# Keys turned by VectorE and moved through DRAM in a two-layer hybrid decoder kernel

## The chip, the cores and the metric

One core of a Trainium2 chip runs the kernel. The metric is device time in microseconds of one execution. The core has TensorE (PE, matrix products, with PEld for loading the stationary operand), VectorE (DVE), ScalarE (ACT), GpSimd (POOL) and SyncE (SP); SP here does nothing but issue transfers (DMAs). PE writes only to PSUM, the other engines work on SBUF and PSUM.

## The reference

Two layers over x (256 tokens, width 1024, f32). Each layer normalises x, projects it by `w_in` to ten parts of 512 columns, runs three branches, multiplies by a SiLU gate and projects back by `w_out`:

```python
h = rms_norm(x, norm_g[l])
q_a, k_a, v_a, q_h, f_h, i_h, q_m, z = split(h @ w_in[l])
qa = partial_rope(rms_norm(q_a), positions); ka = partial_rope(rms_norm(k_a), positions)
o_a = moba_attention(qa, ka, va)       # 8 heads x 64; with 256 tokens one block: causal softmax attention
o_h = rms_norm(hgrn2_chunkwise(q_h, f_h, i_h, lb))           # 4 heads x 128, gated recurrence
k_m, v_m = split(rms_norm(mem) @ w_mem_kv[l])                # 256 memory tokens
o_m = memory_attention(rms_norm(q_m), rms_norm(k_m), v_m)    # 4 heads x 128, softmax
x = x + (concat(o_a, o_h, o_m) * silu(z)) @ w_out[l]
```

All of it is in f32 accuracy.

## The kernel before, in words

**Products.** To get f32 accuracy from fp32r products, both operands of a large product are split into a high and a low part (`wh` by ACT at L161/L164, `wl` by DVE at L173/L176), and three products are summed. A weight chunk is 128 x 1024 (512 KB). It is loaded into one of four raw buffers (`wr`, L136), split into one of three `wh` and `wl` buffers, and used by 12 or 16 products of 512 columns (L215; L1136 for `w_out`). There are 120 chunks in a fixed order: per layer the memory's k and v (8), HGRN's f and q (4 + 4), then k of MoBA, i of HGRN, q of MoBA, the HGRN gate, q of the memory branch, v of MoBA, two more gates (4 each), and `w_out` (12).

**Slots.** The weight products form the backbone. After every six products (in some groups after six and ten) `slot()` is called. It lets each side job, a Python generator, go one step; `yield n` means that a job comes back after n slots. So the order in which the program is written out follows the products. From that order the framework's scheduler sets the order on each engine by a simulated timeline; only the products written with `mm_row`, the loads of weights and a few others are kept in program order among themselves.

**Side jobs that matter here.**
- `g_km` normalises the memory's keys in `kn` (buffer tag `qk`, one buffer, used next by `kr` of MoBA's k) at L600. PE then turns them in two groups of four transposes (L611) into PSUM; ACT takes the high part `kmh` (L612), DVE the low part `kml` (L613). `g_mem_unit` reads them as the moving operand of its scores (12 fp32r products of 256 columns per unit, two units per layer).
- `g_qk` normalises and rotates MoBA's k and q in `kr`; k is scaled at L909, both are turned by PE at L919 and copied out by ACT at L920, into `kT` and `qT`.
- `g_moba` computes the first scores (L219, 8 products of 128 columns and 4 of 256) and starts two units. `g_moba_unit` computes for the second unit its own scores (4 products of 256), takes exps (L967), and passes the probabilities `P` to `across`.
- `across` is the way that P goes already: DVE turns 32 x 32 blocks (L92) into `blk`, one store brings `blk` to a DRAM tile `there` (L96), and four loads bring it back (L99) so that the blocks stand where a full transpose wants them, as `PT`. The columns of PT are in the order (partition quarter, head and token half, 32 tokens), so the PV products read it in runs of 32 columns (L994).
- `room`, `take` and `rel` count buffers: four PSUM tiles `sd` for side products, two buffers `P`, one each of `PTh`, `PTl` and `blk`. The memory units wait for `P`, then for `sd`, then for `PTh` and `PTl`.
- `g_hgrn` runs the recurrence in several levels: DVE scales (L760, L761, L777), PE multiplies in small products (L219).

**SP's queue.** SP issues transfers in order. The weight loads, each waiting until its raw buffer is free, share it with the stores and loads of `across`.

Of the kernel before, what the change touches and what calls it, by code (L numbers as in the profile page):

```python
# [12 lines left out]
F32 = mybir.dt.float32  # L13
F32R = mybir.dt.float32r
# [31 lines left out]
def hymba_kernel(ctx: ExitStack, tc: tile.TileContext, x, mem, mem_t, positions, w_in, w_out, w_mem_kv,  # L46
                 gains, moba_g, out):
    nc = tc.nc
# [15 lines left out]
    def room(what, n=1):  # L64
        while held[what] + n > room_of[what]:
            yield
# [9 lines left out]
    def side_tile():  # L76
        held["sd"] += 1
        assert held["sd"] <= 4
        return psum.tile([128, 512], F32, name="sd", tag="sd", bufs=4)

    def rel(what="sd", n=1):
        held[what] -= n
# [2 lines left out]
        return sb.tile([128, n], F32, name=name, tag=name, bufs=2)  # L85


    def across(dst, src, n):
        yield from room("blk")
        held["blk"] += 1  # L90
        blk = sb.tile([128, 4, n * 32], F32, name="blk", tag="blk", bufs=1)
        nc.vector.transpose(blk.rearrange("p c (n i) -> p c n i", n=n),  # L92
                            src.rearrange("p (n c i) -> p c n i", n=n, c=4))
        yield 2
        there = away.tile([4, 32, 4, n * 32], F32, name="there", tag="there", bufs=2)
        nc.sync.dma_start(there.rearrange("q j c r -> (q j) c r"), blk)  # L96
        yield 2
        for c in range(4):
            nc.sync.dma_start(dst[c * 32:c * 32 + 32], there[:, :, c].rearrange("q j r -> j q r"))  # L99
            if c % 2:  # L100
                yield
        rel("blk")

    chunks = []

# [473 lines left out]
    def g_km(l, acc):  # L579
        ss = small("ssk", 8)  # L580
        kn = sb.tile([128, 2, 512], F32, name="kn", tag="qk", bufs=1)
        nc.vector.tensor_copy(kn[:, 0], acc[0])
        nc.scalar.copy(kn[:, 1], acc[1])  # L583
        yield
        for t in range(2):
            sumsq(ss[:, t * 4:t * 4 + 4], kn[:, t], 4)
        yield
        while "rm" not in done:
            yield
        ms = small("msk", 8)  # L590
        for t in range(2):
            nc.vector.tensor_scalar(ms[:, t * 4:t * 4 + 4], ss[:, t * 4:t * 4 + 4], rm2[:, t:t + 1], EPS,
                                    op0=OP.mult, op1=OP.add)
        r = small("rk", 8)
        nc.gpsimd.tensor_tensor(r, ms, pw[:, :8], op=OP.pow)
        for t in range(2):
            nc.gpsimd.tensor_scalar(r[:, t * 4:t * 4 + 4], r[:, t * 4:t * 4 + 4], rm[:, t:t + 1], None, op0=OP.mult)
        yield 3
        for t in range(2):
            nc.vector.tensor_tensor(heads(kn[:, t], 4), heads(kn[:, t], 4),  # L600
                                    r[:, t * 4:t * 4 + 4][:, :, None].to_broadcast([128, 4, 128]), op=OP.mult)
        yield 3
        kmh = sb.tile([128, 4, 256], F32R, name="kmh", tag="kmh", bufs=1)
        kml = sb.tile([128, 4, 256], F32R, name="kml", tag="kml", bufs=1)
        g = gkq[:, l:l + 1]
        for t in range(2):
            ts = slice(t * 128, (t + 1) * 128)
            yield from room("sd")
            pt = side_tile()
            for h in range(4):  # L610
                nc.tensor.transpose(pt[:, h * 128:(h + 1) * 128], kn[:, t, h * 128:(h + 1) * 128], ident)  # L611
            nc.scalar.activation(kmh[:, :, ts], heads(pt, 4), AF.Copy, scale=g)  # L612
            nc.vector.scalar_tensor_tensor(kml[:, :, ts], in0=heads(pt, 4), scalar=g, in1=kmh[:, :, ts].bitcast(F32),  # L613
                                           op0=OP.mult, op1=OP.subtract)
            rel()
        T["km"] = kmh, kml
        done.add(f"km{l}")

# [259 lines left out]
    def g_qk(l, q, acc):  # L878
        ss = small("ssa", 16)
        ms = small("msa", 16)  # L880
        r = small("rka" if q else "rqa", 16)
        kr = sb.tile([128, 2, 512], F32, name="kr", tag="qk", bufs=1)
        for t in range(2):
            t8 = slice(t * 8, t * 8 + 8)
            sumsq(ss[:, t8], acc[t], 8)
            nc.vector.tensor_scalar(ms[:, t8], ss[:, t8], 1.0 / 64, EPS, op0=OP.mult, op1=OP.add)
            nc.gpsimd.tensor_tensor(r[:, t8], ms[:, t8], pw[:, :8], op=OP.pow)
            a3 = heads(acc[t], 8)
            k3 = heads(kr[:, t], 8)
            nc.vector.tensor_tensor(k3, a3, rtA[:, l, q, t][:, None, :].to_broadcast([128, 8, 64]), op=OP.mult)  # L890
            tm = sb.tile([128, 8, 16], F32, name="tm", tag="tm", bufs=2)
            nc.vector.tensor_tensor(tm[:, :, 0:8], a3[:, :, 8:16],
                                    rtB[:, l, q, t][:, None, 0:8].to_broadcast([128, 8, 8]), op=OP.mult)
            nc.vector.tensor_tensor(tm[:, :, 8:16], a3[:, :, 0:8],
                                    rtB[:, l, q, t][:, None, 8:16].to_broadcast([128, 8, 8]), op=OP.mult)
            yield
            nc.vector.tensor_tensor(k3[:, :, 0:16], k3[:, :, 0:16], tm, op=OP.add)
            yield
        if q == 0:
            rq = small("rq", 16)  # L900
            nc.gpsimd.tensor_scalar(rq, r, 0.125, None, op0=OP.mult)
            nr = small("nr", 16)
            nc.gpsimd.tensor_scalar(nr, r, -0.125, None, op0=OP.mult)
            T["rq"], T["nr"] = rq, nr
        else:
            yield
            for t in range(2):
                k3 = heads(kr[:, t], 8)
                nc.vector.tensor_tensor(k3, k3, r[:, t * 8:t * 8 + 8][:, :, None].to_broadcast([128, 8, 64]),  # L909
                                        op=OP.mult)  # L910
                yield
        yield 2
        tg = ("qT", "kT")[q]
        o = sb.tile([128, 4, 256], F32, name=tg, tag=(f"yl{M_}", f"yh{M_}")[q], bufs=1)
        for t in range(2):
            yield from room("sd")
            pt = side_tile()
            for p in range(4):
                nc.tensor.transpose(pt[:, p * 128:(p + 1) * 128], kr[:, t, p * 128:(p + 1) * 128], ident)  # L919
            nc.scalar.copy(o[:, :, t * 128:(t + 1) * 128], heads(pt, 4))  # L920
            rel()
            yield
        T[tg] = o
        if q == 0:
            spawn(g_moba(l))
# [10 lines left out]
    def second(u):  # L936
        qT, kT = T["qT"], T["kT"]
        ps = [side_tile() for _ in range(2)]
        for pi in range(2):
            for e in range(2):  # L940
                mm_row(ps[e][:, pi * 256:(pi + 1) * 256], qT[64 * e:64 * e + 64, 2 * u + pi, 128:256],
                       kT[64 * e:64 * e + 64, 2 * u + pi])
        return ps

    def second_masked(u, ps, P, mx):
# [5 lines left out]
    def g_moba_unit(l, u, P, mx):  # L951
# [26 lines left out]
        tag = ("PTh", "PTl")[u]  # L978
        yield from take(tag)
        PT = sb.tile([128, 4, 384], F32, name="PT", tag=tag, bufs=1)  # L980
        yield from across(PT, P.rearrange("p i s -> p (i s)"), 12)
        rel("P")
        yield 5
        while f"va{l}" not in done or f"z{A_}{l}" not in done:
            yield
        va = T["va"]
# [13 lines left out]
    def g_moba(l):  # L1000
        T.pop(f"y{A_}", None)
        qT, kT = T["qT"], T["kT"]
        yield
        yield from room("P", 2)
        held["P"] += 2
        P = [sb.tile([128, 4, 384], F32, name="P", tag="P", bufs=2) for _ in range(2)]
        mx = [small("mxa%d" % u, 8) for u in range(2)]

        yield from room("sd", 4)
        ps = [side_tile() for _ in range(2)]  # L1010
        for p in range(4):
            for e in range(2):
                mm_row(ps[e][:, p * 128:(p + 1) * 128], qT[64 * e:64 * e + 64, p, 0:128],
                       kT[64 * e:64 * e + 64, p, 0:128])
        ps1 = second(0)
        yield
        for p in range(4):
            for e in range(2):
                masked(P[p // 2], p % 2 * 2 + e, 0, ps[e][:, p * 128:(p + 1) * 128], mx[p // 2])
        rel("sd", 2)  # L1020
        second_masked(0, ps1, P[0], mx[0])
        for u in range(2):
            yield 1 + 2 * u
            spawn(g_moba_unit(l, u, P[u], mx[u]))


# [28 lines left out]
    def g_mem_unit(l, u, qm, r, nr):  # L1055
# [7 lines left out]
        for t in range(2):  # L1063
            for i in range(2):
                for a, b in passes:
                    mm(ps[t][:, i * 256:(i + 1) * 256], qm[a][:, 2 * u + i, t * 128:(t + 1) * 128],
                       km[b][:, 2 * u + i], (a, b) == passes[0], (a, b) == passes[2])
        yield
        mx = small("mxm%d" % u, 4)
        nb = small("nbm%d" % u, 4)  # L1070
# [181 lines left out]
```

## Time and profile before

| What | Value |
|---|---|
| Median of 3 runs | 402.9 us (402.66 to 403.1) |
| Profiled execution | 402.69 us, span 400.9 us, granted PE clock 1.00 |
| PE, DVE, ACT, POOL busy | 394.4, 309.7, 266.1, 56.7 us |
| DMA | 74.06 MB, 185 GB/s mean |

A row of the groups gives line, engine, operation, what it writes and reads, shape and count, then busy time and the mean of one in ns, then the idle time before the group with what ended it. A row of the chain gives start, duration and what ran. A wait reads "who waits <- for whom: total, times, longest".

### The profile page before, as it was taken

The numbers are of one execution on the slowest core, as the hardware profiler recorded it, in microseconds if no ns is written. First come the engines' busy times: TensorE is split into PE (matmuls) and PEld (weight loads), VectorE is DVE, ScalarE is ACT, GpSimd is POOL, SyncE is SP. The second block draws the span as 40 slices with busy tenths as digits, with TensorE's granted clock in tenths as the row PEclk, the third lists the DMA queues.
The fourth block names the chain that finished last, engine by engine and source line by source line (L and its number), as shares of the span: only waits on it lengthen the run. The fifth ranks groups of instructions, "written<-read, shape, count | busy, mean of one in ns | idle before, by whom it ended". The sixth has DMA issues, their size and how long they took to land.

```text
span 400.9 us, 7637 instructions
## 1 busy us (share of the span) xinstructions
PE 394.4 (98%) x2919; PEld 330.3 (82%) x2919; DVE 309.7 (77%) x602; ACT 266.1 (66%) x438; POOL 56.7 (14%) x79
## 2 busy tenths in 40 slices
PE   8999999999999999999999999999999999999996
PEld 6888888888788888888888888888888889878885
DVE  4789999977559896885576789799656798789643
ACT  5998746584775969864466676456755868897340
POOL 2013405406001200000000040040150040000000
PEclk9999999999999999999999999999999999999999
DMA  8976453355435779337664555544454285953612
GB/s 287 412 276 230 175 180 138 125 199 206 140 115 205 225 252 221 113 115 239 188 194 160 202 163 202 175 146 159 159 171 146 79 261 213 250 194 107 209 54 105
DMA packets 22629, 74.06 MB, mean 185 GB/s; under 512 B 2752, under 2 KB 5184, under 8 KB 22592
## 3 DMA queue, kind: packets, MB, share of 16 engines
q1 hardware_dynamic: 22304, 73.41, 54.7%
q8 instruction: 23, 0.38, 0.4%
q10 hardware_dynamic: 288, 0.15, 0.2%
q14 instruction: 14, 0.11, 0.1%
HBM read 69.36 MB, written 4.19 MB: 183 GB/s over the span
## 4 chain that ended last, share of the span: by engine, by line
PE 95%; ACT 2%; DMA 1%; SPq 0%; DVE 0%; issue 0%; ACTq 0%; DVEq 0%
PE acc L215 66%; PE acc L1136 16%; PE sd L215 5%; PE sd L219 4%; DMA wr<-in_w_mem_kv_dram 1%; ACT P L1081 1%; PE sd L919 1%; PE sd L428 1%; PE sd L1099 1%; ACT wh L161 0%; PE sd L731 0%; PE sd L611 0%; PE sd L1045 0%; SPq L136 0%; ACT wh L164 0%; DVE xs L1170 0%
## 5 line engine op out<-in xcount | busy, mean ns | idle before, releaser
L173 DVE TENSOR_TENSOR wl<-wr,wh 128x1024 fp32r<-128x1024 f32 x104 | 126.4, 1220 | 49.7 <-ACT wh L161 49.5
L161 ACT CAST wh<-wr 128x1024 fp32r<-128x1024 f32 x104 | 109.0, 1051 | 71.7 <-PE acc L215 52.9
L215 PE MATMUL acc<-wh,hT 128*128 128x512 f32 x384 | 126.3, 397 | 0.0
L215 PEld LDWEIGHTS acc<-wh,hT 128*128 128x128 f32 x384 | 72.0, 188 | 16.0 <-issue 0.7
L215 PE MATMUL acc<-wl,hT 128*128 128x512 f32 x192 | 75.1, 391 | 0.0
L215 PE MATMUL acc<-hT,wh 128*128 128x512 f32 x256 | 65.5, 395 | 0.0
L215 PEld LDWEIGHTS acc<-hT,wh 128*128 128x128 f32 x256 | 45.9, 189 | 8.4 <-ACT kn L583 0.4
L215 PEld LDWEIGHTS acc<-wl,hT 128*128 128x128 f32 x192 | 36.1, 188 | 6.7
L1136 PE MATMUL acc<-wl,yh 128*128 128x512 f32 (+1 forms) x96 | 37.2, 387 | 0.0
L215 PEld LDWEIGHTS acc<-hT,wl 128*128 128x128 f32 x256 | 34.8, 190 | 2.5 <-issue 0.3
L1136 PE MATMUL acc<-wh,yl 128*128 128x512 f32 (+1 forms) x96 | 36.8, 387 | 0.0
L215 PE MATMUL acc<-hT,wl 128*128 128x256 f32 x256 | 36.2, 283 | 0.0
L1136 PE MATMUL acc<-wh,yh 128*128 128x512 f32 (+1 forms) x96 | 31.5, 389 | 0.0
L164 ACT ACTIVATE wh<-wr,gT 128x1024 fp32r<-128x1024 f32 (+1 forms) x21 | 19.4, 945 | 9.8 <-PE acc L215 4.0
L215 PE MATMUL acc<-wh,mTh 128*128 128x512 f32 x64 | 25.2, 396 | 0.4 <-ACT wh L164 0.2
L176 DVE SCALAR_TENSOR_TENSOR wl<-wr,gT,wh 128x1024 fp32r<-128x1024 f32 (+1 forms) x21 | 21.0, 1027 | 5.7 <-ACT wh L164 5.5
L215 PE MATMUL acc<-wh,mTl 128*128 128x512 f32 x64 | 24.8, 390 | 0.0
L967 ACT ACTIVATE P<-P,nba,rq 128x128 f32<-128x128 f32 (+1 forms) x32 | 17.1, 538 | 7.1 <-DVE nba L961 7.1
L1136 PEld LDWEIGHTS acc<-wh,yl 128*128 128x128 f32 x96 | 18.0, 188 | 3.7
L1136 PEld LDWEIGHTS acc<-wl,yh 128*128 128x128 f32 x96 | 18.0, 188 | 3.6
L1136 PEld LDWEIGHTS acc<-wh,yh 128*128 128x128 f32 x96 | 17.9, 188 | 3.5
L215 PE MATMUL acc<-wl,mTh 128*128 128x512 f32 x64 | 20.2, 392 | 0.0
(221 smaller groups left out, 584.4 us busy)
## 6 DMA issues: line engine op xcount, KB each, us to landing
wr<-in_w_in_dram SPq DMA_DIRECT2D x80, 512.0 KB, 3.3
wr<-in_w_out_dram SPq DMA_DIRECT2D x24, 512.0 KB, 4.4
wr<-in_w_mem_kv_dram SPq DMA_DIRECT2D x15, 512.0 KB, 4.6
there<-blk SPq DMA_DIRECT2D x4, 768.0 KB, 3.5
PT<-there SPq DMA_DIRECT2D x16, 192.0 KB, 5.9
xs<-in_x_dram SPq DMA_DIRECT2D x2, 512.0 KB, 8.9
memr<-in_mem_dram SPq DMA_DIRECT2D x2, 512.0 KB, 6.7
out_dram<-xs SPq DMA_DIRECT2D x3, 256.0 KB, 2.0
```

Of the source, the lines that this page charges most:

```text
L161: nc.scalar.copy(whs[i], raws[i])
L164: nc.scalar.activation(whs[i][:, sl], raws[i][:, sl], AF.Copy, scale=gT[:, g:g + 1])
L173: nc.vector.tensor_tensor(wls[i], raws[i], whs[i].bitcast(F32), op=OP.subtract)
L176: ins = nc.vector.scalar_tensor_tensor(wls[i][:, sl], in0=raws[i][:, sl], scalar=gT[:, g:g + 1], in1=whs[i][:, sl].bitcast(F32), op0=OP.mu ...
L215: nc.tensor.matmul(o, lhsT=a, rhs=b, start=s, stop=e)
L219: tc.keep_in_program_order(nc.tensor.matmul(o, lhsT=a, rhs=b, start=True, stop=True))
L428: ins = nc.tensor.transpose(pt[:, j * 256 + t * 128:j * 256 + (t + 1) * 128], xn[t][:, k * 128:(k + 1) * 128], ident)
L919: nc.tensor.transpose(pt[:, p * 128:(p + 1) * 128], kr[:, t, p * 128:(p + 1) * 128], ident)
L967: nc.scalar.activation(P[:, i, kc[t]], P[:, i, kc[t]], AF.Exp, bias=nb[:, c:c + 1], scale=rq[:, r:r + 1], accum_out=sm[:, c:c + 1])
L1081: nc.scalar.activation(P[:, t, i], ps[t][:, i * 256:(i + 1) * 256], AF.Exp, bias=nb[:, c:c + 1], scale=r[:, cr:cr + 1], accum_out=sm[:, c: ...
L1099: nc.tensor.transpose(pt[:, i * 256 + t * 128:i * 256 + (t + 1) * 128], P[:, t, i, b * 128:(b + 1) * 128], ident)
L1136: ins = nc.tensor.matmul(a, lhsT=y, rhs=wt[:, cs], start=n == (0 if to is None else nk - 2) and j == 0, stop=n == nk - 1 and j == 2)
```

## The change

1. `kn` isn't turned by PE any more. DVE turns its 32 x 32 blocks, the result goes through DRAM and comes back into `kn` itself (`turned`); then one ACT instruction of 1024 columns makes `kmh` and one DVE instruction makes `kml`.
2. MoBA's k goes the same way into `kT`; q is still turned by PE.
3. Columns of `kmh`, `kml` and `kT` are now in the order (token quarter, token half, head, 32 tokens). The scores pick them by `strips`, in runs of 32 columns, so that the scores themselves stand as before.
4. `across` gives its buffers back sooner: `P` after DVE's transpose, `blk` after the store is written out. Between store and loads there are 4 slots instead of 2, and the four loads go out in two steps.
5. The second MoBA unit starts one slot after the first instead of three, which is twelve products earlier.

```diff
-    def across(dst, src, n):
-        yield from room("blk")
-        held["blk"] += 1
-        blk = sb.tile([128, 4, n * 32], F32, name="blk", tag="blk", bufs=1)
+    def across(dst, src, n, stage=None, free=None):
+        if stage is None:
+            yield from room("blk")
+            held["blk"] += 1
+        tag = stage or "blk"
+        blk = sb.tile([128, 4, n * 32], F32, name="blk", tag=tag, bufs=1)
         nc.vector.transpose(blk.rearrange("p c (n i) -> p c n i", n=n),
                             src.rearrange("p (n c i) -> p c n i", n=n, c=4))
+        if free is not None:
+            rel(free)
         yield 2
         there = away.tile([4, 32, 4, n * 32], F32, name="there", tag="there", bufs=2)
         nc.sync.dma_start(there.rearrange("q j c r -> (q j) c r"), blk)
-        yield 2
+        if stage is None:
+            rel("blk")
+        yield 4
         for c in range(4):
             nc.sync.dma_start(dst[c * 32:c * 32 + 32], there[:, :, c].rearrange("q j r -> j q r"))
-            if c % 2:
+            if c == 1:
                 yield
-        rel("blk")
+
+    def turned(a, stage=None):
+        yield from across(a.rearrange("p (q r) -> p q r", q=4), a, 8, stage)
+        yield 5
+
+    def strips(a):
+        return a.rearrange("p (q t h i) -> p h t q i", q=4, t=2, h=4)
...
@@ g_km
-        kmh = sb.tile([128, 4, 256], F32R, name="kmh", tag="kmh", bufs=1)
-        kml = sb.tile([128, 4, 256], F32R, name="kml", tag="kml", bufs=1)
+        kmh = sb.tile([128, 1024], F32R, name="kmh", tag="kmh", bufs=1)
+        kml = sb.tile([128, 1024], F32R, name="kml", tag="kml", bufs=1)
         g = gkq[:, l:l + 1]
-        for t in range(2):
...
-                nc.tensor.transpose(pt[:, h * 128:(h + 1) * 128], kn[:, t, h * 128:(h + 1) * 128], ident)
-            nc.scalar.activation(kmh[:, :, ts], heads(pt, 4), AF.Copy, scale=g)
-            nc.vector.scalar_tensor_tensor(kml[:, :, ts], in0=heads(pt, 4), ...)
-            rel()
+        flat = kn.rearrange("p t s -> p (t s)")
+        yield from turned(flat)
+        nc.scalar.activation(kmh, flat, AF.Copy, scale=g)
+        nc.vector.scalar_tensor_tensor(kml, in0=flat, scalar=g, in1=kmh.bitcast(F32), op0=OP.mult, op1=OP.subtract)
...
@@ g_qk
+        flat = kr.rearrange("p t s -> p (t s)")
+        o = sb.tile([128, 1024], F32, name=tg, tag=(f"yl{M_}", f"yh{M_}")[q], bufs=1)
+        if q == 0:
...
+        else:
+            yield from across(o.rearrange("p (q r) -> p q r", q=4), flat, 8)
+            yield 5
...
@@ second
-                mm_row(ps[e][:, pi * 256:(pi + 1) * 256], qT[64 * e:64 * e + 64, 2 * u + pi, 128:256],
-                       kT[64 * e:64 * e + 64, 2 * u + pi])
+                mm_row(ps[e][:, pi * 256:(pi + 1) * 256].rearrange("p (t q i) -> p t q i", t=2, q=4),
+                       qT[64 * e:64 * e + 64, 2 * u + pi, 128:256], strips(kT)[64 * e:64 * e + 64, 2 * u + pi])
...
@@ g_moba_unit
-        yield from across(PT, P.rearrange("p i s -> p (i s)"), 12)
-        rel("P")
-        yield 5
+        yield from across(PT, P.rearrange("p i s -> p (i s)"), 12, free="P")
+        yield 6
...
@@ g_moba
-                mm_row(ps[e][:, p * 128:(p + 1) * 128], qT[64 * e:64 * e + 64, p, 0:128],
-                       kT[64 * e:64 * e + 64, p, 0:128])
+                mm_row(ps[e][:, p * 128:(p + 1) * 128].rearrange("p (q i) -> p q i", q=4),
+                       qT[64 * e:64 * e + 64, p, 0:128], strips(kT)[64 * e:64 * e + 64, p, 0])
...
         for u in range(2):
-            yield 1 + 2 * u
+            yield
             spawn(g_moba_unit(l, u, P[u], mx[u]))
...
@@ g_mem_unit
-                    mm(ps[t][:, i * 256:(i + 1) * 256], qm[a][:, 2 * u + i, t * 128:(t + 1) * 128],
-                       km[b][:, 2 * u + i], (a, b) == passes[0], (a, b) == passes[2])
+                    mm(ps[t][:, i * 256:(i + 1) * 256].rearrange("p (t q s) -> p t q s", t=2, q=4),
+                       qm[a][:, 2 * u + i, t * 128:(t + 1) * 128], strips(km[b])[:, 2 * u + i],
+                       (a, b) == passes[0], (a, b) == passes[2])
```

More of the change, by code (lines that the diff above doesn't have):

```diff
@@ L602, in g_km @@
         yield 3
-        kmh = sb.tile([128, 4, 256], F32R, name="kmh", tag="kmh", bufs=1)
-        kml = sb.tile([128, 4, 256], F32R, name="kml", tag="kml", bufs=1)
+        kmh = sb.tile([128, 1024], F32R, name="kmh", tag="kmh", bufs=1)
+        kml = sb.tile([128, 1024], F32R, name="kml", tag="kml", bufs=1)
         g = gkq[:, l:l + 1]
-        for t in range(2):
[L607 to L611, printed above, removed]
-            nc.scalar.activation(kmh[:, :, ts], heads(pt, 4), AF.Copy, scale=g)
-            nc.vector.scalar_tensor_tensor(kml[:, :, ts], in0=heads(pt, 4), scalar=g, in1=kmh[:, :, ts].bitcast(F32),
-                                           op0=OP.mult, op1=OP.subtract)
-            rel()
+        flat = kn.rearrange("p t s -> p (t s)")
+        yield from turned(flat)
+        nc.scalar.activation(kmh, flat, AF.Copy, scale=g)
+        nc.vector.scalar_tensor_tensor(kml, in0=flat, scalar=g, in1=kmh.bitcast(F32), op0=OP.mult, op1=OP.subtract)
         T["km"] = kmh, kml
@@ L913, in g_qk @@
         tg = ("qT", "kT")[q]
[L914 to L922, printed above, removed]
+        flat = kr.rearrange("p t s -> p (t s)")
+        o = sb.tile([128, 1024], F32, name=tg, tag=(f"yl{M_}", f"yh{M_}")[q], bufs=1)
+        if q == 0:
+            o = o.rearrange("p (h s) -> p h s", h=4)
+            for t in range(2):
+                yield from room("sd")
+                pt = side_tile()
+                for p in range(4):
+                    nc.tensor.transpose(pt[:, p * 128:(p + 1) * 128], kr[:, t, p * 128:(p + 1) * 128], ident)
+                nc.scalar.copy(o[:, :, t * 128:(t + 1) * 128], heads(pt, 4))
+                rel()
+                yield
+        else:
+            yield from across(o.rearrange("p (q r) -> p q r", q=4), flat, 8)
+            yield 5
         T[tg] = o
@@ L1022, in g_moba @@
         for u in range(2):
-            yield 1 + 2 * u
+            yield
             spawn(g_moba_unit(l, u, P[u], mx[u]))
@@ L1065, in g_mem_unit @@
                 for a, b in passes:
-                    mm(ps[t][:, i * 256:(i + 1) * 256], qm[a][:, 2 * u + i, t * 128:(t + 1) * 128],
-                       km[b][:, 2 * u + i], (a, b) == passes[0], (a, b) == passes[2])
+                    mm(ps[t][:, i * 256:(i + 1) * 256].rearrange("p (t q s) -> p t q s", t=2, q=4),
+                       qm[a][:, 2 * u + i, t * 128:(t + 1) * 128], strips(km[b])[:, 2 * u + i],
+                       (a, b) == passes[0], (a, b) == passes[2])
+        done.add(f"scores{u}{l}")
         yield
```

## The prediction, made before the change was run

> **What bounds the kernel now.** I read the page first (busy times, then the chain that ended last), then the chain piece by piece, the groups by shape, busy time by stage, the timelines of VectorE (DVE) and TensorE (PE) around the weakest place, and the DMA queue's waits.
>
> ```profile
> span 400.9 us, 7637 instructions
> PE 394.4 (98%) x2919; PEld 330.3 (82%) x2919; DVE 309.7 (77%) x602; ACT 266.1 (66%) x438; POOL 56.7 (14%) x79
> ...
> PE 95%; ACT 2%; DMA 1%; SPq 0%; DVE 0%; issue 0%; ACTq 0%; DVEq 0%
> ```
>
> PE is busy nearly without a break and 95% of the chain is PE, so a product taken off PE shortens the run by its own time, as long as nobody else becomes late. The profiled execution took 402.69 us with a span of 400.9; the median of the runs is 402.9, 0.2 above it. About 0.2% (0.8 us) is what a measurement of this kernel can tell from no change.
>
> The chain in order of time shows the products that go and those whose operand is laid out anew:
>
> ```profile
> 44.85 0.87 PE sd L611 x8
> ...
> 80.38 0.44 PE sd L919 x4
> 80.82 1.39 PE acc L215 x6
> 82.21 0.44 PE sd L919 x4
> ...
> 86.74 0.88 PE sd L219 x63
> ...
> 107.40 1.96 PE sd L219 x24
> ...
> 138.63 1.43 PE sd L215 x12
> ...
> 153.36 1.50 PE sd L215 x16
> ```
>
> Columns: start, duration in us, what. Six weight products are one slot of the kernel's schedule, 1.39 us. Both layers together have (count | busy us, mean ns of one | idle before):
>
> ```profile
> L919 PE MATMUL sd<-ident,kr 128*128 128x128 f32 x32 | 4.8, 272 | 0.0
> ...
> L611 PE MATMUL sd<-ident,kn 128*128 128x128 f32 x16 | 2.1, 272 | 0.0
> ```
>
> **Part 1: the transposes that leave PE.** Per layer 8 of kn (L611) and 8 of MoBA's k (L919, the first two groups of four; of L919's 32, 16 are q's and stay). By the chain 0.87 + 0.44 + 0.44 = 1.75 in the first layer, and as many of the same length in the second: **-3.50 us**. All lie on the chain. This is the one large term.
>
> **Part 2: what takes their place.**
>
> ```profile
> L176 DVE SCALAR_TENSOR_TENSOR wl<-wr,gT,wh 128x1024 fp32r<-128x1024 f32 x11 | 13.8, 1280 | 3.2 <-ACT wh L164 3.1
> ...
> L92 DVE STREAM_TRANSPOSE blk<-P 128x1536 f32<-128x1536 f32 x4 | 7.1, 1768 | 0.0
> ```
>
> A DVE transpose of 1024 columns: 1.77 x 1024/1536 = 1.18 us (estimate from L92). Per layer DVE gets two of them and one kml of 1024 columns (1.28, as L176) in place of two half as long: some +2.4 us. ACT makes kmh in one instruction instead of two of half the columns, and loses the two copies of kT: less work on an engine that is 66% busy, 0. DVE's addition isn't on the chain by its sum either (77% busy); what counts is where it falls (part 4).
>
> The Trainium skill, "VectorE: DVE Perf Modes", section "Rules for kernel authors", speaks against the change: a 128x128 transpose belongs on TensorE if PSUM will do as the target. By that rule the transposes are better left where they are, and the time would be 402.9 or more; the trace has PE full and DVE with idle time, so I go by the rows.
>
> **Part 3: the way through DRAM.** Per layer two stores of 512 KB and eight loads of 128 KB each go onto SP's queue on top, 4.2 MB in all beside 74.06 MB.
>
> The rows are the DMA issues (KB each, us to landing), ACT's preparation of weights with what ended its idle time, and SP's longest wait (total, times, longest), and the loads of the first PT (start, duration of the issues):
>
> ```profile
> there<-blk SPq DMA_DIRECT2D x4, 768.0 KB, 3.5
> PT<-there SPq DMA_DIRECT2D x16, 192.0 KB, 5.9
> ```
>
> ```profile
> L161 ACT CAST wh<-wr 128x1024 fp32r<-128x1024 f32 x104 | 109.0, 1051 | 71.7 <-PE acc L215 52.9 <-PE acc L1136 15.5 <-ACT wh L161 1.8
> ```
>
> ```profile
> SPq L136 <- DVE wl L173: 177.8, 62, 7.8
> ```
>
> ```profile
> 128.25 1.75 SPq L99 DMA_DIRECT2D PT<-there  x4
> ```
>
> k has time. From the place of its transposes the new code counts 2 slots to the store, 4 to the first loads, 1 to the last, 5 to the end. kT: 80.4 + 7 x 1.39 + 5.9 = 96 us, needed by the scores at 107.4: eleven us of cover, 0. kn: loads issued by 54.6, landed by 60.5; km is used at 138.6, but kn's buffer is wanted by kr at 67.5 (part 4). Without that cover each us of lateness is one of PE's.
>
> SP issues in order, so the weight loads stand behind the new stores and loads. A store waits for its DVE transpose, a load for its store's landing (3.5 us, covered by 4 slots = 5.6). SP now waits 2.9 us (177.8/62) before a weight load for DVE to free a buffer, and ACT's wh waited for PE, never for the DMA: the weights lie there early. So 0; if the cover were gone, each us that SP is blocked beyond it would stop PE for one. The same holds for the two slots more between the P store and its loads (PT's loads start at 128.25, land in 5.9, and the PV products stand at 153.4) and for P and blk given back earlier.
>
> **Part 4: the place without slack.** DVE's timeline, then PE's, first layer; then the same two of the second layer (start, duration):
>
> ```profile
> 67.52 0.67 DVE L890 TENSOR_TENSOR kr<-acc,rtA 128x512 f32<-128x512 f32 x1
> ...
> 77.28 1.22 DVE L173 TENSOR_TENSOR wl<-wr,wh 128x1024 fp32r<-128x1024 f32 x1
> ```
>
> ```profile
> 79.06 0.40 PE L215 MATMUL acc<-wl,hT 128*128 128x512 f32 x1
> ```
>
> ```profile
> 272.65 3.49 DVE L173 TENSOR_TENSOR wl<-wr,wh 128x1024 fp32r<-128x1024 f32 x3
> ```
>
> ```profile
> 274.83 0.40 PE L215 MATMUL acc<-wl,hT 128*128 128x512 f32 x1
> ```
>
> ```profile
> 50.00:64.00 14.00, 14.00 (x189) 11.64 (x188) 12.42 (x37) 7.56 (x11) 0.34 (x2) 1.00 0.54 188
> 64.00:78.00 14.00, 14.00 (x244) 11.32 (x243) 13.40 (x28) 8.48 (x12) 9.46 (x17) 1.00 0.34 115
> 154.00:164.00 10.00, 9.23 (x68) 7.58 (x65) 7.39 (x17) 9.92 (x19) 0.00 (x0) 1.00 0.65 204
> 250.00:264.00 14.00, 14.00 (x186) 11.49 (x185) 10.94 (x19) 7.44 (x10) 0.00 (x0) 1.00 0.45 154
> 350.00:360.00 10.00, 9.23 (x67) 7.56 (x63) 7.54 (x17) 9.92 (x19) 0.00 (x0) 1.00 0.67 209
> ```
>
> Columns after the stretch and its length: PE, PEld, DVE, ACT, POOL busy, with counts; granted clock (1.00), DMA share, GB/s. From 64 to 78 us DVE works 13.40 of 14 us, and the weight remainder wl that ends at 78.50 is read by PE at 79.06: 0.56 us of slack, 0.96 in the second layer (273.87 against 274.83; three of 1.22 in the row's stretch). kml, now made right after the transposes (44.85), can only be made after the loads, from about 61 us, and must be done before kr (67.5). In 50 to 64 DVE idles 1.58 us, in 250 to 264 3.06 us: made there, it costs nothing. Made after 64 it pushes wl by 1.28: a stall of 0.72 and 0.32. If k's transpose (1.18) also goes ahead of that wl: 1.90 and 1.50, together 3.40. PE's gain of 0.87 before this place doesn't eat the slack, for this stretch of DVE starts from what PE delivers. Below nothing I see no reason. Bounds 0 to 3.40; I take **+0.5**, half of the kml case, since the idle time before is nearer to the landing.
>
> k's transpose itself stands behind that wl and the two after it, as L919 does now: 77.28 + 3 x 1.22 + 1.18 = 82.1 or a little later, 4.6 us before the HGRN products at 86.74 whose operands DVE makes in between. I take 0; if they need it all, 1.18 per layer, inside the 3.40.
>
> **Part 5: strided products.** Scores now read k in runs of 32 columns. The PV products already read PT in such runs: 153.36, 16 instructions, 8 of 256 and 8 of 128 columns, 1.50/3072 = 0.488 ns per column; today's contiguous scores at 107.40 have 4096 columns in 1.96, 0.479. So f32 pays nothing. The memory scores are fp32r, contiguous at 138.63: 1.43/3072 = 0.466. No row has fp32r strided; the transposes' rate, 0.44/512 = 0.86, is the far end: 48 products x 256 x 0.39 = 4.8 us. I take 0, since two PV products share the array (128x64 each) and so together already read strided columns at nearly the fp32r rate. The Trainium skill, "SBUF — State Buffer", section "Specifications (TRN2)", gives full bandwidth from two accesses per 16-byte line on; runs of 128 bytes do, so by it the price is 0 as well, and no run here shows fp32r.
>
> **Part 6: second unit's scores, P free earlier.** The scores go up by two slots, 2.8 us. Four masking steps go with them on DVE; the work only comes sooner, 0. P given back earlier lets the second memory unit begin sooner. That bears on the only hole in PE: in 154 to 164 and 350 to 360 PE idles 0.77 us each, where this row stands:
>
> ```profile
> PE sd L1099 <- ACT P L1081: 0.8, 2, 0.4
> ```
>
> The transposes of the first memory unit wait for PSUM tiles that the second unit's exps still read. If those exps come sooner, the hole closes: 0 to -1.54. What could be late instead is the softmax's table switching on ACT. I take **-0.8**, half.
>
> **Sum.** -3.50 + 0.5 - 0.8 = -3.8: 402.69 to 398.9, on the scale of the median 399.1.
>
> **The rivals.** *The hole closes and DVE costs nothing*: -5.04, 397.9. For it: exps that start earlier; against: ACT is busy 9.92 of 10 us there.
> *DVE becomes the bound at 64 to 79*: kml alone without the closed hole 402.9 - 3.50 + 1.04 = 400.4; with k's transpose ahead of wl 402.8, no change. For it: 0.56 us of slack; against: idle time just before.
> *Strided fp32r is slow* (other side): 402.9 - 3.5 + 4.8 = 404.2. It decides from 0.466 + 3500/12288 = 0.75 ns per column on. For it: no row; against: the PV rate.
> *The DRAM trip blocks SP's queue*, a store waiting behind a late transpose: slower once the weights come more than 3.5 us late in sum. For it: ten more issues per layer in an ordered queue; against: SP's 2.9 us in reserve.
> *The scores don't move*, because other work still holds the two PSUM tiles they need: no time either way, inside the first case.
> A rule that would give another time: the Trainium skill, "VectorE: DVE Perf Modes", section "The three transpose paths", calls a plain DMA that transposes by strides 19 times slower. As an estimate 19 x 5.9 = 112 us per load would put kT some 90 us behind its use in each layer, near 580 us. The P loads of the same kind land in 5.9 us, in runs of many elements, so I give it less than 1 in 100.
>
> **How the numbers follow.** 0.42 for the sum, 0.20 for the closed hole, 0.16 for 400.4, 0.10 for 402.8, 0.07 for 404.2, 0.05 for a blocked queue. Faster 0.78 (the first three), same 0.10, slower 0.12. The range starts under the closed hole, 397.5, and ends at 402.0, past 400.4; outside lie the last three, about 0.2.
>
> **What would show it.** No L611 group of four, 16 instead of 32 at L919; PE busy near 391; L161 still waiting for PE, never for wr; kml between 58 and 66; wl before the q products over 0.3 ahead of PE; memory scores still 1.43 for 12; PE 10.00 of 10 where 154 to 164 was. Wrong: PE waiting for DVE at about 77 or 272, DMA as a releaser of wh, memory scores above 2.3.

## The result, and the profile after

The changed kernel takes 399.03 us (median; 398.48 to 400.0), the kernel before took 403.0 beside it: ratio 0.9896, interval 0.9871 to 0.9921, 4.0 us faster. The prediction was 399.1. The profiled execution took 399.08 us, 3.61 less than that of before. In the changed file the numbers are shifted: L215 is L227, L219 is L231, L161/L173 are L173/L185, L919 is L928, L1099 is L1112, L1136 is L1149.

The page of the changed kernel (span; busy times; shares of the chain):

```profile
span 397.3 us, 7614 instructions
...
PE 391.6 (99%) x2887; PEld 326.9 (82%) x2887; DVE 312.2 (79%) x604; ACT 258.4 (65%) x428; POOL 53.0 (13%) x79
...
PE 86%; DVE 6%; DMA 3%; POOL 2%; issue 1%; ACT 1%; SPq 0%; DVEq 0%; ACTq 0%
```

32 products fewer, PE 2.8 us less busy, and PE's share of the chain down from 95% to 86%: something else sets the end for a while. To find where, I take one landmark that both chains have in both layers, the first transposes of q. Before, then after:

```profile
101.00 0.44 PE sd L919 x4
...
296.83 0.44 PE sd L919 x4
```

```profile
100.81 0.44 PE sd L928 x4
...
294.15 0.44 PE sd L928 x4
```

Up to the first landmark all of the first layer's key transposes (1.75 us) are gone, yet only 0.19 us is won: **1.56 us are lost on the way**. Between the landmarks 2.49 us are won: 1.75 from the second layer's transposes, 0.74 from elsewhere. From the second landmark to the end of the span another 0.92. Together -0.19 - 2.49 - 0.92 = -3.60.

Busy time by stage (stretch, length; PE, PEld, DVE, ACT, POOL; clock, DMA share, GB/s), first a stretch of before that the prediction doesn't show, then the changed kernel:

```profile
72.00:90.00 18.00, 18.00 (x266) 14.61 (x265) 15.11 (x24) 13.42 (x24) 3.42 (x1) 1.00 0.47 155
```

```profile
72.00:90.00 18.00, 16.88 (x255) 13.34 (x254) 17.34 (x31) 11.28 (x20) 5.69 (x18) 1.00 0.46 154
154.00:164.00 10.00, 10.00 (x71) 8.77 (x71) 9.67 (x17) 8.76 (x14) 0.00 (x0) 1.00 0.43 149
264.00:278.00 14.00, 14.00 (x242) 11.56 (x229) 13.40 (x24) 7.12 (x10) 4.25 (x2) 1.00 0.55 185
350.00:360.00 10.00, 10.00 (x71) 9.00 (x67) 9.25 (x15) 7.48 (x13) 0.00 (x0) 1.00 0.45 156
```

Both holes of PE at 154 and 350 are closed. A new one of 1.12 us stands at 72 to 90, in the first layer alone; at the same place of the second layer PE is busy 14.00 of 14. The waits of PE and of its weight loads (total, times, longest) name what came late:

```profile
PE acc L227 <- DVE wl L185: 0.6, 1, 0.6
PE sd L231 <- DVE hKb L767: 0.5, 1, 0.5
```

```profile
PEld acc L1149 <- DVE wl L185: 1.0, 2, 0.5
PEld acc L227 <- DVE wl L185: 0.9, 1, 0.9
```

The first wait is for the weight remainder that the prediction watched (77.28 in the kernel before). In the changed kernel DVE makes it here:

```profile
77.65 1.21 DVE L185 TENSOR_TENSOR wl<-wr,wh 128x1024 fp32r<-128x1024 f32 x1
```

It ends at 78.86, only 0.36 us later than before, which the slack of 0.56 us would have covered. But PE, rid of kn's transposes, now wants it sooner: in the fastest version below, where it doesn't wait, it reads this remainder at 78.20 instead of 79.06. Here PE idles 0.58 us until 78.92. All of the 1.56 us are lost between 77 and 88 us; 1.12 of them are idle time of PE, the other 0.44 don't show in its busy share.

The chain of the changed kernel tells why DVE is late (start, duration in us):

```profile
43.23 1.15 DVE blk L94
44.41 2.96 DMA there<-blk
...
48.71 5.80 DMA kn<-there
54.61 1.16 ACT kmh L620
55.80 1.28 DVE kml L621
57.09 0.09 DVE rt L491
...
74.25 0.73 POOL rtA L533
...
75.92 0.39 DVE kr L896
...
83.94 1.16 DVE blk L94
...
85.93 0.69 DVE hKb L767
...
86.75 0.65 PE sd L231 x32
```

From kn's DVE transposition to its return in SBUF 11 us pass. The timelines show who stands behind it: the sine of the rotary table on ACT and what runs on POOL, before, then kmh and sine (ACT), kml (DVE) and POOL's work in the changed kernel (the last bracket is the engine's idle time just before):

```profile
63.35 0.23 ACT L510 ACTIVATE sc<-rt 128x32 f32<-128x32 f32 x1
...
63.66 0.22 POOL L521 TENSOR_TENSOR rtA<-sc,mg 128x16 f32<-128x16 f32 x1 [18.29 <-ACT sc L510]
```

```profile
54.61 1.15 ACT L620 ACTIVATE kmh<-kn,gkq 128x1024 fp32r<-128x1024 f32 x1 [2.36 <-DMA kn<-there]
71.72 0.23 ACT L522 ACTIVATE sc<-rt 128x32 f32<-128x32 f32 x1 [1.91 <-DVE rt L521]
...
55.80 1.28 DVE L621 SCALAR_TENSOR_TENSOR kml<-kn,gkq,kmh 128x1024 fp32r<-128x1024 f32 x1 [2.03 <-ACT kmh L620]
...
69.78 4.47 POOL L893 TENSOR_TENSOR rka<-msa,pw 128x8 f32<-128x8 f32 x2 [25.41 <-DVE rt L498]
```

Each engine works in the order that the scheduler fixed. ACT idles 2.36 us for the DMA, and DVE 2.03 us for `kmh`, which waits for the same loads. The small instructions that reduce the rotary angles (rt) stand behind kml on DVE, so the sine comes at 71.7 instead of 63.4; on POOL the two powers of rka (4.47 us) now stand ahead of rtA; and kr, which needs rtA, starts at 75.92 instead of 67.5. The weight remainders and the HGRN operands that follow on DVE then reach PE too late; ahead of the HGRN operand `hKb` the chain also has k's own DVE transposition (`blk` at 83.94). The second layer has no such stall. The table is made only once, and the wait for kn is shorter there too (0.8 us on ACT, 0.4 us on DVE).

**Theory**: the stall is the wait for kn's return, passed on through the table. **Rivals**: k's trip causes it; DVE's extra work or the DMA traffic does; or kml pushes wl directly, as the prediction had it. For the holes: they close because P is free sooner, because the second MoBA unit comes sooner, or because fewer products stand on PE.

### The profile page after: what moved, and what is told of

The parts are those of the page before. It is cut to its first block, busy times and chain, and to the rows that moved or that the text cites. A ratio compares the mean times of both kernels' runs of the same rounds, so it can differ in the third digit from the quotient of the medians.

```text
span 397.3 us, 7614 instructions
## 1 busy us (share of the span) xinstructions
PE 391.6 (99%) x2887; PEld 326.9 (82%) x2887; DVE 312.2 (79%) x604; ACT 258.4 (65%) x428; POOL 53.0 (13%) x79
## 4 chain that ended last, share of the span: by engine, by line
PE 86%; DVE 6%; DMA 3%; POOL 2%; issue 1%; ACT 1%; SPq 0%; DVEq 0%; ACTq 0%
PE acc L227 58%; PE acc L1149 15%; PE sd L227 6%; PE sd L231 3%; DVE wl L185 2%; DMA kn<-there 1%; POOL rka L893 1%; PE sd L1112 1%; PE sd L440 1%; DMA gT<-in_gains_dram 1%; DMA there<-blk 1%; DVE blk L94 1%; ACT wh L173 1%; PE sd L737 0%; PE sd L1056 0%
## 5 line engine op out<-in xcount | busy, mean ns | idle before, releaser
L185 DVE TENSOR_TENSOR wl<-wr,wh 128x1024 fp32r<-128x1024 f32 x104 | 126.3, 1218 | 41.2 <-ACT wh L173 41.2
L173 ACT CAST wh<-wr 128x1024 fp32r<-128x1024 f32 x104 | 108.9, 1051 | 67.9 <-PE acc L227 37.2
L227 PE MATMUL acc<-wh,hT 128*128 128x512 f32 x384 | 124.8, 396 | 0.0
L227 PEld LDWEIGHTS acc<-wh,hT 128*128 128x128 f32 x384 | 71.8, 188 | 16.0 <-issue 0.7
L227 PE MATMUL acc<-wl,hT 128*128 128x512 f32 x192 | 75.2, 392 | 0.6 <-DVE wl L185 0.6
L227 PE MATMUL acc<-hT,wh 128*128 128x512 f32 x256 | 66.0, 395 | 0.0
L227 PEld LDWEIGHTS acc<-hT,wh 128*128 128x128 f32 x256 | 45.7, 189 | 8.6 <-ACT kn L595 0.4
L227 PEld LDWEIGHTS acc<-wl,hT 128*128 128x128 f32 x192 | 36.1, 188 | 7.8 <-DVE wl L185 0.9
L1149 PE MATMUL acc<-wl,yh 128*128 128x512 f32 (+1 forms) x96 | 37.4, 390 | 0.1
L227 PEld LDWEIGHTS acc<-hT,wl 128*128 128x128 f32 x256 | 35.1, 190 | 2.6
L1149 PE MATMUL acc<-wh,yl 128*128 128x512 f32 (+1 forms) x96 | 37.2, 388 | 0.0
L227 PE MATMUL acc<-hT,wl 128*128 128x256 f32 x256 | 36.4, 282 | 0.0
L1149 PE MATMUL acc<-wh,yh 128*128 128x512 f32 (+1 forms) x96 | 29.8, 388 | 0.0
L227 PE MATMUL acc<-wh,mTh 128*128 128x512 f32 x64 | 25.5, 401 | 0.2 <-DVE mTh L379 0.2
L227 PE MATMUL acc<-wh,mTl 128*128 128x512 f32 x64 | 24.8, 390 | 0.0
L1149 PEld LDWEIGHTS acc<-wl,yh 128*128 128x128 f32 x96 | 18.0, 188 | 4.4 <-DVE wl L185 1.0
L1149 PEld LDWEIGHTS acc<-wh,yh 128*128 128x128 f32 x96 | 17.9, 188 | 3.9 <-ACT wh L173 0.4
L1149 PEld LDWEIGHTS acc<-wh,yl 128*128 128x128 f32 x96 | 18.0, 188 | 3.6
L227 PE MATMUL acc<-wl,mTh 128*128 128x512 f32 x64 | 20.2, 392 | 0.0
```

The costliest lines, as they stand in the source:

```text
L173: nc.scalar.copy(whs[i], raws[i])
L185: nc.vector.tensor_tensor(wls[i], raws[i], whs[i].bitcast(F32), op=OP.subtract)
L227: nc.tensor.matmul(o, lhsT=a, rhs=b, start=s, stop=e)
L1149: ins = nc.tensor.matmul(a, lhsT=y, rhs=wt[:, cs], start=n == (0 if to is None else nk - 2) and j == 0, stop=n == nk - 1 and j == 2)
```

## The experiments

Every ratio is against the kernel before, timed on the same chip.

**One part at a time.** Only kn by DRAM, all else as before:

```
 g_qk, scores, second unit, P:   as before
 g_km, memory scores:            as changed
```

> Only kn goes through DRAM; MoBA's k is turned by PE as before, the second unit, P and the slots are as before. Theory (the first layer's stall at 75 to 87 us comes from kn's return, which holds ACT and DVE and pushes the one-time rotary tables back): 402.9 - 1.74 (16 transposes) + 1.4 (stall, first layer only) = 402.5, and PE idles about 1.1 us between 72 and 90. Rival (the stall comes from k's own DVE transpose in that place): 402.9 - 1.74 = 401.2 and no idle time there.

402.07 us (401.41 to 404.64), ratio 0.999 (0.9973 to 1.0007), so not clear of no change. Only MoBA's k by DRAM:

```
 g_km, memory scores, second unit, P:   as before
 g_qk, MoBA's scores:                   as changed
```

> Only MoBA's k goes through DRAM; kn, the second unit, P and the slots are as before. Theory: 402.9 - 1.76 = 401.1, PE without idle time between 72 and 90. Rival (k's DVE transpose makes the first layer's stall): 402.6 and idle time there.

400.72 us, 0.9951 (0.9938 to 0.9965). Both keys, the rest as before (`across_p` is the `across` of the kernel before):

```
...
-        yield from across(PT, P.rearrange("p i s -> p (i s)"), 12, free="P")
-        yield 6
+        yield from across_p(PT, P.rearrange("p i s -> p (i s)"), 12)
+        rel("P")
+        yield 5
...
-            yield
+            yield 1 + 2 * u
```

> Both keys go through DRAM; the second unit, P, blk and the slots of P's trip are as before. Theory: 402.9 - 3.5 + 1.4 = 400.8 with both holes of 0.77 us there. Rival (the holes close without the unit's part): 399.2.

400.18 us, 0.994 (0.9917 to 0.9964). And the reverse, both keys on PE with the second unit sooner, P and blk given back sooner, 4 slots:

> Both keys are turned by PE as before; the second unit's earlier scores, P and blk given back sooner and the 4 slots stay. Theory (these close the hole of 0.77 us per layer near 160 and 355): 402.9 - 1.5 = 401.4. Rival (the hole closes because PE arrives earlier without the transposes): 402.9 and 0.77 us idle in each hole.

401.65 us, 0.9967 (0.9955 to 0.9979). The stretch from 72 to 90, kn only, k only, both keys, and the stretch of the hole for the last kernel:

```profile
72.00:90.00 18.00, 17.55 (x262) 13.95 (x262) 15.55 (x28) 13.16 (x24) 4.93 (x17) 1.00 0.42 141
```

```profile
72.00:90.00 18.00, 18.00 (x262) 14.57 (x261) 15.72 (x25) 12.18 (x22) 3.42 (x1) 1.00 0.66 204
```

```profile
72.00:90.00 18.00, 17.47 (x258) 14.20 (x257) 17.16 (x30) 11.86 (x22) 5.09 (x18) 1.00 0.47 158
```

```profile
154.00:164.00 10.00, 10.00 (x73) 8.56 (x70) 9.63 (x18) 8.85 (x14) 0.00 (x0) 1.00 0.47 157
```

The stall belongs to kn's trip: it is there with kn alone and not with k alone, whose DMA share is the higher (0.66). So k's trip alone doesn't make it, and this speaks against traffic. Once the table is late, k's transposition does take part: with both keys PE's only wait there is 0.5 us for hKb, which DVE makes behind it, while with kn alone PE waits 0.4 us for kr. The stall is smaller than expected in both kernels, 0.45 and 0.53 us of idle time against 1.1, and their times are 0.4 and 0.6 us under the theory. PE's idle time follows the time at which kmh can start, and with it kr: 53.86 and 75.16 us, 0.45 us idle (kn only); 54.02 and 75.32, 0.53 (both keys); 54.61 and 75.92, 1.12 (the changed kernel). The holes stay when only keys move (9.23 to 9.26 of 10) and close with the other part alone. Medians: -0.8, -2.1 and -1.2 make -4.1; the whole gave -4.0.

**The link in the chain.** The three long stages of the angle reduction work on a tile of their own that nobody reads, so the sine no longer waits for them. The same edit in the kernel before is the control.

```
...
+        keep = kf, an
+        aside = sb.tile([128, 4, 2 * HALF], F32, name="aside")
+        nc.vector.tensor_copy(aside[:, 3], an)
+        kf, an = aside[:, 0:3], aside[:, 3]
         periods(0, 22, 0.0)
...
+        kf, an = keep
```

> The changed kernel, but the three long stages that reduce the rotary angles work on a tile of their own that nobody reads, and sine and cosine are taken of the unreduced angles (that part of the computation is left out; DVE does one small copy more, none less). The trip of kn, its wait and its 1.28 us kml stay. Theory (the wait for kn's return hurts through the rotary table, which is pushed back and reaches kr late): sine starts before 65 us instead of 71.7, PE busy at least 17.7 of 18 us between 72 and 90, 397.5 us (397.0 to 398.2). Rival (kml and the wait push the weight remainders wl directly, as the prediction had it): PE still idle 0.7 us or more between 72 and 90, 398.6 to 399.3.

> The kernel before with the same edit to the rotary angles as in the changed kernel with unreduced angles (three reduction stages on a tile nobody reads; that part of the computation is left out). Before the change the table was ready in time, so both theories: PE busy 18.00 of 18 between 72 and 90 as before, no difference, 402.5 to 403.2. If it were 1 us or more faster, the table's chain costs time in itself, and the comparison with the changed kernel would say nothing on the trip.

The changed kernel: 397.94 us, 0.986 (0.9836 to 0.9884). The kernel before: 402.88 against 402.94, 0.9991 (0.9976 to 1.0006), PE busy 18.00 of 18 as ever. Timeline and stretch of the changed kernel with this edit:

```profile
54.15 0.23 ACT L528 ACTIVATE sc<-rt 128x32 f32<-128x32 f32 x1
...
66.90 0.68 DVE L902 TENSOR_TENSOR kr<-acc,rtA 128x512 f32<-128x512 f32 x1
```

```profile
72.00:90.00 18.00, 18.00 (x261) 14.62 (x260) 16.08 (x28) 12.58 (x22) 2.24 (x1) 1.00 0.68 216
```

kml stands nearly where it did, at 55.45, and DVE has no less to do, but the stall is gone with 1.1 us. So it runs through the table; kml doesn't push wl directly. The edit does more than undo the lateness: the sine now comes 9 us earlier than in the kernel before, and DVE idles 0.87 us ahead of kml instead of 2.03.

The intervals of this kernel, of the next one and of the one with the table begun sooner overlap with that of the changed kernel. The 1.0 to 1.2 us between their medians therefore rest on the profiles as well: spans of 396.2, 396.1 and 395.8 us against 397.3, and PE's idle time between 72 and 90.

**The wait itself.** kn's loads land in a buffer that nobody reads:

```
     def turned(a, stage=None):
-        yield from across(a.rearrange("p (q r) -> p q r", q=4), a, 8, stage)
+        back = sb.tile([128, 1024], F32, name="back", tag="back", bufs=1)
+        yield from across(back.rearrange("p (q r) -> p q r", q=4), a, 8, stage)
```

> The changed kernel, but kn's four loads land in a buffer that nobody reads, and kmh and kml are made from the unturned kn (MoBA's memory keys are then not turned: that part of the computation is left out). Store, loads, DVE's transpose, kmh and kml all stay with their sizes; only the wait of ACT and DVE for the DMA is gone. Theory (the wait is the cost): no wait of 2 us before kmh and kml, PE busy at least 17.7 of 18 between 72 and 90, 397.5 us (397.0 to 398.2). Rival (DVE's extra work or the extra DMA traffic is the cost): stall stays, 398.6 to 399.3.

398.04 us, 0.9878 (0.9854 to 0.9902). The sine comes at 70.54, kr at 74.74. The stretch:

```profile
72.00:90.00 18.00, 17.80 (x260) 14.36 (x259) 16.57 (x29) 12.22 (x22) 4.51 (x17) 1.00 0.47 165
```

With transfers and DVE's work all kept, 1.0 us comes back, and 0.9 of the 1.12 us of idle time. So neither the traffic nor the amount of DVE's work is the cost. But kml moves too, from 55.80 to 44.40, out of the way of the small instructions; the wait and the place of kml weren't separated. And sine and kr are only 1.2 us earlier. Most of the sine's 8.4 us of lateness is therefore not the wait but the order in which the small instructions now stand; the wait, with kml behind it, is what takes the last slack. How much each of the two orders (rt on DVE, rka ahead of rtA on POOL) gives wasn't separated.

**kml on POOL**, so that DVE reads nothing that kn's loads bring:

```
-        nc.vector.scalar_tensor_tensor(kml, in0=flat, scalar=g, in1=kmh.bitcast(F32), ...)
+        nc.gpsimd.tensor_scalar(flat, flat, g, None, op0=OP.mult)
+        nc.gpsimd.tensor_tensor(kml, flat, kmh.bitcast(F32), op=OP.subtract)
```

> The changed kernel, but POOL makes kml in two instructions of 1024 columns (kn times its gain, then minus kmh) instead of DVE in one; nothing is left out. POOL idled from 43 to 69 us. DVE then stands behind no DMA, and has 1.28 us less work in each layer. Theory: rotary table as early as before the change (sine near 63 us), PE busy at least 17.7 of 18 between 72 and 90, 397.5 us (396.9 to 398.2), the fastest version so far. Rival (POOL's two instructions are slow enough, over 8 us, to hold back the table's products on POOL itself or the buffer of kn): 399 to 401.

400.42 us (398.66 to 402.3), 0.9928 (0.9902 to 0.9955): by the medians slower than the change (the intervals overlap), and a miss: the theory's 397.5 isn't reached. The profiled execution is the slowest of the seven, so its places count here, not its total. ACT's `kmh`, POOL's second instruction and DVE's:

```profile
56.09 1.15 ACT L620 ACTIVATE kmh<-kn,gkq 128x1024 fp32r<-128x1024 f32 x1 [3.68 <-DMA kn<-there]
...
60.29 3.44 POOL L622 TENSOR_TENSOR kml<-kn,kmh 128x1024 fp32r<-128x1024 f32 x1
...
57.79 1.20 DVE L685 TENSOR_TENSOR hQ<-as,sg 128x512 f32<-128x512 f32 x1 [3.25 <-ACT sg L683]
58.92 0.16 DVE L498 SCALAR_TENSOR_TENSOR rt<-rt 128x16 f32<-128x16 f32 x1
...
61.39 2.57 DVE L498 SCALAR_TENSOR_TENSOR rt<-rt 128x16 f32<-128x16 f32 x2
```

Two things hold DVE up. It still stands behind the DMA, through another engine: ACT idles 3.68 us for kn, `sg` stands behind `kmh` on ACT, and DVE idles 3.25 us for `sg`. And two instructions of 16 columns, 0.16 us for one elsewhere, last until POOL is done. How much each gives wasn't separated. The sine came at 72.77, later than in the changed kernel: the rival's time was right, and POOL does hold the table back, but by blocking DVE and not by its own length (6.3 us, under the 8 expected), and not alone. The Trainium skill, "SBUF — State Buffer", section "SBUF: two separate sides", says that DVE and GpSimd share a pair of ports, that an instruction locks it for its whole length, and that the other engine blocks. The rows beside POOL's second instruction agree. Beside its first (2.86 us from 57.34) they don't: the instruction of 16 columns at 58.92 took 0.16 us there, and one of 1024 columns with two inputs (59.03) the usual 1.23.

**The table begun sooner**, nothing left out:

```
     def g_loads():
-        while "hT0" not in done:
+        while "mraw" not in done:
...
-        while "hT0" not in done:
+        while "mraw" not in done:
             yield
         pf = small("pf", 2)
...
-        rt = sb.tile([128, 8, 2 * HALF], F32, name="rt", tag="hX", bufs=1)
+        rt = sb.tile([128, 8, 2 * HALF], F32, name="rt", tag="rt", bufs=1)
```

> The changed kernel, whole, with the rotary table begun sooner: positions and gains are loaded, and the angles begun, as soon as the memory's halves are split (about 14 us) instead of when the first layer's input is normalised (about 31 us); the angles get a tile of their own. The trip of kn, its wait and kml stay. Theory (kn's wait costs by pushing the table): sine before 62 us, PE 17.7 of 18 or more between 72 and 90, 397.7 us (397.2 to 398.3). Rival (the small DVE instructions now fall between the normalised input's, on which the first products wait): the gain of 1.1 us at 75 to 87 is given back before 40 us, 399 to 400.

397.84 us, 0.9882 (0.9863 to 0.9901). The sine comes at 63.01. The stretch:

```profile
72.00:90.00 18.00, 17.78 (x259) 14.26 (x258) 15.72 (x25) 11.25 (x21) 3.42 (x1) 1.00 0.66 207
```

The sine is 1 us later than expected, but where it was before the change, and 1.2 us are won. kn's trip is still there, and ACT still idles 1.47 us for it; kml now stands at 59.26, so late that DVE doesn't idle for it.

**What closes the holes.** The kernel before with P and blk given back sooner alone, and with the second MoBA unit sooner alone (the diff of the change, first `across` and `free="P"`, then `yield` for `yield 1 + 2 * u`):

> The kernel before with one part of the change alone: P is given back right after DVE's transposition and blk after its store, with 4 slots between store and loads. Both keys stay on PE, and the second MoBA unit starts where it did. Theory A (the hole at 154 to 164 closes because P is free sooner and so the second memory unit starts sooner): PE 10.00 of 10 there, 401.6 us (401.3 to 401.9), all of the 1.2 us of the two parts together. Theory B (it closes because the second MoBA unit comes sooner): hole of 0.75 us stays in both layers, 402.6 to 403.1.

> The kernel before with the other part alone: the second MoBA unit starts two slots sooner; P, blk and the slots between store and loads as before, both keys on PE. Theory A: the second unit still waits for P or the PSUM tiles, and the hole at 154 to 164 stays, 402.6 to 403.1 us. Theory B: PE 10.00 of 10 there, 401.6 us (401.3 to 401.9). If both parts alone give half each, neither does it without the other.

400.8 us, 0.9948 (0.9932 to 0.9963), and 400.67, 0.9944 (0.993 to 0.9959). Neither theory foresaw this: either part closes both holes by itself (PE busy 10.00 of 10 from 154 to 164 and from 350 to 360, in both kernels), and each alone is worth 2.0 to 2.1 us, both together 1.2. The kernel with both was timed on another chip; the intervals overlap at their edges, the runs don't (401.48 to 401.68 us against 400.32 to 401.12).

What both together have, and neither alone has, is the 0.5 us in each layer that a weight load of the output products (L1149 of the changed kernel) waits for wl.

**The best of it**: table sooner, P free sooner, the second unit where it was.

```
-            yield
+            yield 1 + 2 * u
             spawn(g_moba_unit(l, u, P[u], mx[u]))
```

> The changed kernel, whole, with the rotary table begun sooner (397.84 us by itself) and the second MoBA unit started where it did before the change, so that of the two parts that each closed the hole alone (400.80 and 400.67 against 401.65 for both) only P's early release is left. Theory (both together cost 0.9 us more than either, at the place where the weight load of the output products waits 0.5 us for wl in each layer): that wait gone, PE still 10.00 of 10 in 154 to 164, 397.0 us (396.6 to 397.5). Rival (the 0.9 us between those runs belongs to the place of k's scores while the keys are turned on PE): no change, 397.6 to 398.3.

397.29 us (396.68 to 399.05), 0.9863 (0.9835 to 0.989): the fastest version, 0.55 below the one above by the medians, whose intervals overlap. The chains and spans bear it out. The landmark of q with the table sooner alone (span 395.8), then here (span 394.9):

```profile
99.35 0.44 PE sd L928 x4
...
292.68 0.44 PE sd L928 x4
```

```profile
99.23 0.44 PE sd L928 x4
...
292.14 0.44 PE sd L928 x4
```

Landmark to landmark 193.33 against 192.91, landmark to the end 103.12 against 102.76: 0.4 us in each layer, and the wait of L1149 is no longer in the list. All six kernels here with both parts have this wait (1.0 us in all), the three with one part haven't. By the medians one part alone is faster by 0.55 us (the last two kernels) to 1.0 us (with the keys on PE). That the wait is the whole of this difference isn't shown. Which of DVE's instructions makes wl late there wasn't tried.

## Why the prediction was right, step by step

The time, 399.1 against 399.03, is right, and the case held likeliest gave it. That it agrees to 0.1 us is luck: two terms were off, part 4 by +1.06 us and part 6 by -0.86, and nearly cancel. Two of the signs of being wrong that the prediction named came true: PE waits for DVE at about 77, and DMA is among the releasers of wh.

*Part 1, -3.50*: right. The second layer shows its half, with no term against it: 2.49 us won between the landmarks, where PE waits for nothing at the place of the first layer's stall. k alone gave 2.1 us (1.4 to 2.5 by its interval) for its 1.75.

*Part 2, 0*: right on sizes (DVE's transposition 1.23 us against an estimate of 1.18, kml 1.28). The place of this work is part 4.

*Part 3, 0 for DRAM and SP's queue*: right for k. The changed kernel's issues (KB each, median us to landing):

```profile
there<-blk SPq DMA_DIRECT2D x4, 512.0 KB, 3.2
...
kn<-there SPq DMA_DIRECT2D x8, 128.0 KB, 4.6
kT<-there SPq DMA_DIRECT2D x8, 128.0 KB, 4.4
```

No load lands 19 times late. The factor of the Trainium skill, "VectorE: DVE Perf Modes", section "The three transpose paths", compares with the DMA's own transpose and is for a large innermost destination stride. The prediction's 112 us took a plain load of P for its base, so that estimate doesn't follow from it. Weights stay ahead, nearly: DMA ends some of the wait of the changed L173, 2.2 us in all, where the prediction had "never" (and had left out L164, where DMA ended 2.4 us already before). PE's products name no wait for wh of that line; its weight loads do, 0.4 us at the output products. kn was loaded as soon as the store landed (47.4 to 48.7), and back at 54.5, not 60.5: the scheduler moves the issues up, so the slots between store and loads set nothing here. By the rule of the Trainium skill, "VectorE: DVE Perf Modes", section "Rules for kernel authors" (128x128 transposes on TensorE), the time would have stayed at 403; the measurement decides against it for a kernel in which PE is the bound.

*Part 4, +0.5*: **the step that failed**. The place was right (wl and the HGRN operands late for PE at about 77 in the first layer), the size was not: +1.56 in the first layer and 0 in the second. The sentence that failed is that kml, made in DVE's idle time before 64 us, costs nothing. It was made there, at 55.8, even sooner than the 61 us that the prediction counted with. But kmh and kml already stood at the head of two engines' queues while their operand was on its way, and the work behind them was not wl but the table, which the prediction hadn't looked at. Slack was read at the end of the stretch, for one instruction, instead of along the queue. Two more steps failed with it. "PE's gain of 0.87 before this place doesn't eat the slack" is wrong: wl came 0.36 us later and PE wanted it 0.86 us sooner, because this stretch of DVE was now set by the table and not by what PE delivers. And k's transposition, put at 0, stands on the chain ahead of hKb, for which PE waits 0.5 us.

*Part 5, 0*: nearly right. The twelve memory scores, strided fp32r now, run in two groups of six; each lasts until the next product starts:

```profile
144.18 0.28 PE L227 MATMUL sd<-kml,qmh 128*128 128x256 f32 x1
...
144.90 1.75 PE L227 MATMUL acc<-hT,wh 128*128 128x512 f32 x7
...
146.96 0.29 PE L227 MATMUL sd<-kml,qmh 128*128 128x256 f32 x1
...
147.70 0.64 PE L227 MATMUL acc<-hT,wl 128*128 128x256 f32 x4
```

0.72 + 0.74 = 1.46 us against 1.43 contiguous: at most some 2%, which is near the rounding of these starts. The bound of 4.8 us is far off.

*Part 6, -0.8*: too small. Between the landmarks and behind the second one the profile gives -0.74 and -0.92, in all -1.66, the part alone -1.2 by its median, and one half of it -2.0. The bound of -1.54 counted only PE's idle time; the weight loads of the same products waited too, which the list of before shows:

```profile
PEld sd L1099 <- ACT P L1081: 2.5, 4, 0.7
```

That these waits make up the rest is argued, not shown.

Of the rivals, "the hole closes and DVE costs nothing" would have been 397.9; that is about what the changed kernel gives once the table isn't held back (397.84 and 397.94). "DVE becomes the bound" described the right place and the wrong carrier.

## What to carry to other kernels

An engine works in its fixed order, so an instruction fed by a DMA holds back everything behind it, also work that has nothing to do with it: before moving an operand through DRAM, look not at when its user needs it but at what stands behind the first instruction that reads it, on every engine, and how much slack that has, one-time set-up work included. Where two edits cure the same hole, try each alone: both together can cost more than either. A weight load that waits can be lost time that the busy share of the products doesn't show. And a product taken off the bound engine brings it sooner to the next operand that others make: slack read before the change can be smaller after it.

## What was not expected of the hardware

While POOL ran a two-operand instruction of 1024 columns (3.44 us), two of DVE's two-operand instructions of 16 columns took 2.57 us together instead of 0.16 each; beside POOL's one-operand instruction (2.86 us) one took 0.16 as usual. A DMA that transposes in runs of many elements lands 128 KB in 4.4 to 4.6 us, hardly later than a plain load of weights of 512 KB (4.3). Moving operands of fp32r products in runs of 32 columns cost at most some 2%.
